# Output tiles with stationary weights: wide and narrow matmuls in series, turned about in every second tile

## The chip, the cores and the metric

The kernel runs on one core of one Trainium2 chip. The metric is the device time of one execution in microseconds (us); lower is better. A core has five engines that work side by side and wait for each other through semaphores: PE (matmul), DVE (vector), ACT (scalar), POOL (general) and SP, which issues transfers here. Each of them works its own instructions off in the order in which they stand in the program.

## What is computed

A decoder trunk of two layers over 256 tokens of width 2048, in float32. Each layer normalises its input, projects it with one wide matrix, runs three groups of attention heads over parts of the result, projects back, and adds; then it normalises again and runs a gated MLP with a short causal convolution. A last norm follows.

```python
for l in range(DEPTH):                                   # DEPTH = 2
    h = _rmsnorm(x, attn_norm[l])
    z = jnp.einsum('bsd,de->bse', h, w_in[l])            # 2048 -> 4934
...
    o_a = _diff_attention(a_q, a_k, a_v, ...)            # 4 heads
    o_b = _mla_attention(m_cq, m_ckv, m_kr, ...)         # 6 heads
    o_c = _forgetting_attention(f_q, f_k, f_v, f_g, ...) # 6 heads
    x = x + jnp.einsum('bsm,md->bsd', mix, w_o[l])
    h = _rmsnorm(x, ffn_norm[l])
    x = x + _conv_gated_mlp(h, ffn_w_up[l], ..., ffn_w_down[l])   # D_FF = 5632
return _rmsnorm(x, final_norm)
```

## The kernel before

The weights, some 400 MB, come through one stream of blocks of 128 x 128 numbers, sixteen blocks a transfer (`load`, tile `raw`, three buffers, issued on SP). `convert` turns eight blocks at a time into two operands of the PE's type for rounded float32: ACT casts the block to `hi` (L134), and DVE subtracts that from the original, which leaves the rest `lo` (L135). Each of `hi` and `lo` has four buffers of eight blocks, and a cast into a buffer waits until PE has read the last block out of it. Activations are split the same way: `hx[k]` holds the high part of 256 tokens in its left half and the low part in its right half, 128 x 512 in all.

`mm_t` makes one output tile of 128 features by 256 tokens over the 16 blocks of its inner dimension, with the weights as the stationary operand. For each block it runs a **wide** matmul, `hi` against all 512 columns of `hx[k]` (left half: high by high, right half: high by low), and a **narrow** one, `lo` against the 256 columns of the high part. They alternate: wide, narrow, wide, narrow (L184, L185), and only the last block has the narrow one first (L187, L188). `total` then adds the two halves of the bank: ACT copies one out (L229), DVE adds the other (L231). `mm_t2` makes two output tiles at once in the same way; it is used for the first tiles of a stage, while the operands still come in (L202 to L205). `mm_v` has the activations stationary and moves 512 columns of weights (L220 to L222, all of one width), for values, the output projection and the second half of the MLP (`residual`). `narrow`, in the latent heads, moves 256 columns of activations against stationary weights (L731 to L733).

`weights(b)` hands out the operands of block `b`; at the first block of a buffer it also calls `convert` for that buffer and the next two, and `load` for two chunks ahead. Background work, such as the heads' scores and softmax, is cut into steps (`bg`, `tick`) that are put between tiles. A scheduler in the library sets the order of each engine's instructions from the program text and the dependences; nothing of a time is written down by hand.

At the start the first chunks come in quarters, and ACT and DVE turn about between converting weights and splitting `x` into `hx` (L361, L362). At the end the last `residual` multiplies three of four column groups of x by the final gain on POOL and the fourth on DVE (L817), the sums of squares are reduced (L406), ACT takes the square root (L407, which needs its function table loaded), DVE the reciprocal (L408), and ACT and DVE scale the two token halves and send them out (L825 to L828).

Of the kernel before, what the change touches and what calls it, by code (L numbers as in the profile page):

```python
# [10 lines left out]
F32R = mybir.dt.float32r  # L11
I32 = mybir.dt.int32
AF = mybir.ActivationFunctionType
# [45 lines left out]
def kernel(ctx: ExitStack, tc: tile.TileContext, xin, xnat, pos, wstream, cst, par, fin, out):  # L59
# [11 lines left out]
    def nm(s):  # L71
        uid[0] += 1
        return f"{s}_{uid[0]}"

    def slot(dtype=F32):
        return slots.tile([P, 2 * T], dtype, tag="slot", name=nm("slot"))
# [10 lines left out]
    def bank(tag, bufs):  # L87
        return psum.tile([P, 512], F32, tag=tag, name=nm(tag), bufs=bufs)

    def f(ap):  # L90
        return ap.bitcast(F32)
# [18 lines left out]
    def load_first():  # L110
        for c in range(3):
            t = wpool.tile([P, CH * P], F32, tag="raw", name=nm("raw"), bufs=3)
            src = wflat[c * CH * P * P : (c + 1) * CH * P * P].rearrange("(p e) -> p e", p=P)
            for i in range(4):
                a = slice(i * 4 * P, (i + 1) * 4 * P)
                nc.sync.dma_start(t[:, a], src[:, a])
                if c < 2:
                    nc.sync.dma_start(xg[4 * c + i], xin[4 * c + i])
            raws[c] = t

    def convert(s, between=None):
        if s >= len(bounds) or s in subs:
            return
        at, n = bounds[s]
        c = at // CH
        load(c)
        o = (at - c * CH) * P
        src = raws[c][:, o : o + n * P]
        hi = wpool.tile([P, SUB * P], F32R, tag="hi", name=nm("hi"), bufs=4)
        lo = wpool.tile([P, SUB * P], F32R, tag="lo", name=nm("lo"), bufs=4)  # L130
        step = SUB // 2 * P if c < 3 else SUB * P
        for o in range(0, n * P, step):
            a = slice(o, min(o + step, n * P))
            nc.scalar.copy(hi[:, a], src[:, a])  # L134
            nc.vector.tensor_tensor(lo[:, a], src[:, a], f(hi[:, a]), ALU.subtract)  # L135
            if between is not None:
                between()
        subs[s] = (hi, lo)

    def weights(b, n=1):  # L140
        s = sub_of[b]
        at = bounds[s][0]
        if b == at:
            convert(s)
            convert(s + 1)
            convert(s + 2)
            load(b // CH + 1)
            load(b // CH + 2)
        o = (b - at) * P
        hi, lo = subs[s]  # L150
        return hi[:, o : o + n * P], lo[:, o : o + n * P]
# [20 lines left out]
        while bg or active:  # L172
            tick()

    def mm_t(moving, hooks={}, tag="mm", bufs=3):
        ps = bank(tag, bufs)
        k = len(moving)
        for i, mv in enumerate(moving):
            if i in hooks:
                hooks[i]()  # L180
            hi, lo = weights(cb[0])
            cb[0] += 1
            if i < k - 1:
                nc.tensor.matmul(ps, hi, mv, start=(i == 0), stop=False)  # L184
                nc.tensor.matmul(ps[:, :T], lo, mv[:, :T], start=False, stop=False)  # L185
            else:
                nc.tensor.matmul(ps[:, :T], lo, mv[:, :T], start=(i == 0), stop=False)  # L187
                nc.tensor.matmul(ps, hi, mv, start=False, stop=True)  # L188
        return ps
# [52 lines left out]
    nc.scalar.activation(warm, warm, AF.Square)  # L242
    nc.scalar.dma_start(pr[0][:, :Q_CV], par[0, :, :Q_CV])
    load_first()
    nc.sync.dma_start(cs, cst)
    nc.sync.dma_start(pint, pos)
    nc.sync.dma_start(pr[0][:, Q_CV:], par[0, :, Q_CV:])
# [283 lines left out]
    for l in range(DEPTH):  # L531
# [4 lines left out]
        if l == 0:  # L536
            first = mm_t2(hx)
            convert(4)
            convert(5)
            squares()  # L540
            first.append(mm_t(hx))
            first.append(mm_t(hx, {KT // 2: norm.cols}, "s", 2))
        else:
            first = mm_t2(hx, {4: lambda: norm.turn(3), KT // 2: norm.cols})
        rstd = norm.rows("rstd")
# [230 lines left out]
        for half in range(2):  # L776
            acts = []
            for i in range(HALF):
                ft = half * HALF + i
                ys = []  # L780
                if rstd is None:
                    pair = mm_t2(hx, {4: lambda: norm.turn(3), KT // 2: norm.cols})
                    rstd = norm.rows("rstd")
                else:
                    pair = None
                for j in range(2):
                    u = total(pair[j] if pair else mm_t(hx))
                    uu = tmp()
                    nc.gpsimd.tensor_tensor(uu, u, rstd, ALU.mult)  # L789
                    w = Q_CV + (ft + j * FT) * 4  # L790
                    y = tmp()
                    nc.scalar.activation(y, uu, AF.Identity, scale=q_[:, w + 2 : w + 3], bias=q_[:, w + 3 : w + 4])  # L792
                    nc.vector.scalar_tensor_tensor(y[:, 1:], uu[:, : T - 1], q_[:, w + 1 : w + 2], y[:, 1:], ALU.mult, ALU.add)  # L793
                    nc.vector.scalar_tensor_tensor(y[:, 2:], uu[:, : T - 2], q_[:, w : w + 1], y[:, 2:], ALU.mult, ALU.add)  # L794
                    ys.append(y)
                nc.scalar.activation(ys[1], ys[1], AF.Silu)  # L796
                nc.gpsimd.tensor_tensor(ys[0], ys[0], ys[1], ALU.mult)  # L797
                a = slot(F32R)
                to_hl(a, ys[0])
                acts.append(a)  # L800
            if half == 0:
                residual(acts, 0)
            elif l < DEPTH - 1:
                hx = [big.tile([P, 2 * T], F32R, tag=f"h{k}", name=nm("h")) for k in range(KT)]
                norm = RowNorm(pr[l + 1][:, Q_AN : Q_AN + KT], hx)
                residual(acts, 0, norm.turn)
            else:
                gf = [slot() for _ in range(4)]
                for j in range(4):
                    nc.sync.dma_start(gf[j], fin[:, j * 512 : (j + 1) * 512])  # L810
                norm = RowNorm(None, None)

                def gain(j):
                    a = slice(j * 512, (j + 1) * 512)
                    for t in range(2):
                        e = nc.vector if j == 3 else nc.gpsimd
                        e.tensor_tensor(xr[t][:, a], xr[t][:, a], gf[j], ALU.mult)  # L817

                residual(acts, 0, gain)
                gain(3)  # L820

    col = norm.cols()
    for j in range(4):
        a = slice(j * 512, (j + 1) * 512)
        nc.vector.tensor_scalar(xr[0][:, a], xr[0][:, a], col[:, 0:1], None, ALU.mult)  # L825
        nc.sync.dma_start(out[0][:, a], xr[0][:, a])
        nc.scalar.activation(xr[1][:, a], xr[1][:, a], AF.Copy, scale=col[:, 1:2])
        nc.scalar.dma_start(out[1][:, a], xr[1][:, a])  # L828


def _layout(inputs):
# [129 lines left out]
```

## Time and profile before

| what | value |
|---|---|
| median of three runs | 2270.15 us (2269.72 to 2270.17) |
| profiled execution | 2270.36 us |
| its span, first to last instruction | 2268.6 us |
| PE busy, share of the span | 2248.8 us, 99% |
| DVE, ACT, POOL busy | 1506.2, 1229.3, 385.1 us |
| matmuls | 12072 |
| mean transfer rate | 182 GB/s |

A timeline row has the start in us from the span's beginning, the duration in us, the engine, the line of the kernel, the operation, output and inputs, and how many follow each other; in brackets stands how long the engine was idle before it and what ended that. A group's row has the count, the busy time in us and the mean duration in ns of one. A row of waits has the waiting engine with tile and line, what it waited for, the total in us, the count and the longest. Matmuls overlap in the pipeline, so a matmul's duration is longer than the distance from its start to the next one's; where PE is concerned, starts are compared.

### The profile page before, as it was taken

The page shows a single profiled execution, that of the slowest core. Times are in us where ns is not written, and L with a number is a line of the kernel's source. Part 1 is how long each engine was busy: PE and PEld are TensorE (multiplying, and loading weights), DVE is VectorE, ACT ScalarE, POOL GpSimd, SP SyncE. Part 2 cuts the span into 40 slices and gives each one's busy share as a digit, 9 for nine tenths or more (in the row PEclk, how much of TensorE's full clock was granted, in tenths as well). Part 3 has the DMA queues.
Part 4 walks back from the last instruction along what each step waited for, and adds up shares of the span by engine and source line. Part 5 has one row for each costly group of instructions (what it writes and reads, how often), then busy time and mean ns, then how long its engine had stood idle before and what let it go on. Part 6 is the DMA issues. An engine that isn't in the chain of part 4 may idle for free.

```text
span 2268.6 us, 31133 instructions
## 1 busy us (share of the span) xinstructions
PE 2248.8 (99%) x12072; PEld 1923.5 (85%) x12072; DVE 1506.2 (66%) x2316; ACT 1229.3 (54%) x1866; POOL 385.1 (17%) x395
## 2 busy tenths in 40 slices
PE   8999999999999999999999999999999999999997
PEld 7888978888888888888888888788888888888886
DVE  8768766777754577775574777567777546777654
ACT  7456645655543455554454665456555435555543
POOL 4600000222210122220050100002222001222110
PEclk9999999999999999999999999999999999999999
DMA  8544435555555555555555444345555555555553
GB/s 310 192 154 165 152 141 182 180 187 187 187 194 187 192 187 188 187 188 190 185 186 185 151 166 162 128 177 186 186 186 186 198 191 188 185 188 185 208 197 120
DMA packets 60771, 413.58 MB, mean 182 GB/s; under 512 B 6864, under 2 KB 6992, under 8 KB 11600
## 3 DMA queue, kind: packets, MB, share of 16 engines
q1 hardware_dynamic: 59904, 410.54, 50.2%
q8 instruction: 94, 1.54, 0.3%
q10 hardware_dynamic: 720, 1.07, 0.1%
q14 instruction: 53, 0.43, 0.1%
HBM read 409.49 MB, written 2.10 MB: 181 GB/s over the span
## 4 chain that ended last, share of the span: by engine, by line
PE 98%; DVE 1%; ACT 0%; DMA 0%; issue 0%; POOL 0%; ACTq 0%; SPq 0%; DVEq 0%
PE mm L184 35%; PE mm L185 18%; PE mm L220 12%; PE mm L222 11%; PE mm L221 11%; PE mm L188 2%; PE s L438 2%; PE mm L205 1%; PE mm L187 1%; PE mm L203 1%; PE pv L470 1%; PE s L397 0%; PE mm L731 0%; PE mm L732 0%; PE mm L733 0%; PE pv L471 0%
## 5 line engine op out<-in xcount | busy, mean ns | idle before, releaser
L135 DVE TENSOR_TENSOR lo<-raw,hi 128x1024 fp32r<-128x1024 f32 (+1 forms) x775 | 988.5, 1276 | 520.6 <-ACT hi L134 516.2
L184 PE MATMUL mm<-h,hi 128*128 128x512 f32 x3375 | 1203.9, 399 | 0.0
L134 ACT CAST hi<-raw 128x1024 fp32r<-128x1024 f32 (+1 forms) x775 | 808.2, 1044 | 588.6 <-PE mm L222 379.4
L185 PE MATMUL mm<-h,lo 128*128 128x256 f32 x3375 | 947.1, 281 | 0.0
L184 PEld LDWEIGHTS mm<-h,hi 128*128 128x128 f32 x3375 | 634.1, 188 | 148.5 <-issue 1.7
L185 PEld LDWEIGHTS mm<-h,lo 128*128 128x128 f32 x3375 | 637.1, 189 | 9.5
L220 PE MATMUL mm<-hi,slot 128*128 128x512 f32 x992 | 388.1, 391 | 0.6 <-DVE slot L735 0.6
L221 PE MATMUL mm<-lo,slot 128*128 128x512 f32 x992 | 384.8, 388 | 0.0
L222 PE MATMUL mm<-hi,slot 128*128 128x512 f32 x992 | 384.7, 388 | 0.0
L789 POOL TENSOR_TENSOR tmp<-tmp,rstd 128x256 f32<-128x256 f32 x176 | 133.2, 757 | 1018.6 <-DVE tmp L231 862.3
L220 PEld LDWEIGHTS mm<-hi,slot 128*128 128x128 f32 x992 | 186.3, 188 | 42.5 <-issue 4.0
L222 PEld LDWEIGHTS mm<-hi,slot 128*128 128x128 f32 x992 | 186.3, 188 | 38.3
L221 PEld LDWEIGHTS mm<-lo,slot 128*128 128x128 f32 x992 | 186.4, 188 | 36.9
L229 ACT COPY tmp<-mm 128x256 f32<-128x256 f32 (+1 forms) x233 | 86.6, 372 | 157.1 <-PE mm L188 155.5
L797 POOL TENSOR_TENSOR tmp<-tmp,tmp 128x256 f32<-128x256 f32 x88 | 119.9, 1362 | 262.1 <-ACT tmp L796 262.1
L792 ACT ACTIVATE tmp<-tmp,par 128x256 f32<-128x256 f32 x176 | 105.7, 601 | 72.1 <-POOL tmp L789 72.0
L231 DVE TENSOR_TENSOR tmp<-mm,tmp 128x256 f32<-128x256 f32 (+1 forms) x233 | 97.7, 419 | 51.1 <-ACT tmp L229 51.0
L476 DVE TENSOR_TENSOR slot<-tmp,slot 128x256 fp32r<-128x256 f32 x96 | 40.8, 425 | 92.2 <-ACT slot L475 92.2
L475 ACT CAST slot<-tmp 128x256 fp32r<-128x256 f32 x96 | 39.0, 406 | 107.3 <-POOL tmp L797 105.5
L188 PE MATMUL mm<-h,hi 128*128 128x512 f32 x225 | 89.8, 399 | 0.0
L794 DVE SCALAR_TENSOR_TENSOR tmp<-tmp,par,tmp 128x254 f32<-128x254 f32 x176 | 85.1, 483 | 6.1
L793 DVE SCALAR_TENSOR_TENSOR tmp<-tmp,par,tmp 128x255 f32<-128x255 f32 x176 | 83.3, 474 | 5.3 <-ACT tmp L792 5.3
(183 smaller groups left out, 1692.4 us busy)
## 6 DMA issues: line engine op xcount, KB each, us to landing
raw<-in_w SPq DMA_DIRECT2D x381, 1024.0 KB, 4.8
raw<-in_w SPq DMA_DIRECT2D x12, 256.0 KB, 5.4
slot<-in_x SPq DMA_DIRECT2D x8, 256.0 KB, 5.2
x<-in_xn SPq DMA_DIRECT2D x2, 1024.0 KB, 10.8
slot<-in_fin SPq DMA_DIRECT2D x4, 256.0 KB, 6.3
out<-x SPq DMA_DIRECT2D x4, 256.0 KB, 3.8
out<-x ACTq DMA_DIRECT2D x4, 256.0 KB, 3.8
raw<-in_w SPq DMA_DIRECT2D x1, 512.0 KB, 3.2
```

The source lines that it names most:

```text
L134: nc.scalar.copy(hi[:, a], src[:, a])
L135: nc.vector.tensor_tensor(lo[:, a], src[:, a], f(hi[:, a]), ALU.subtract)
L184: nc.tensor.matmul(ps, hi, mv, start=(i == 0), stop=False)
L185: nc.tensor.matmul(ps[:, :T], lo, mv[:, :T], start=False, stop=False)
L188: nc.tensor.matmul(ps, hi, mv, start=False, stop=True)
L220: nc.tensor.matmul(ps[t][:, :n], s_hi, hi, start=(i == 0), stop=False)
L221: nc.tensor.matmul(ps[t][:, :n], s_hi, lo, start=False, stop=False)
L222: nc.tensor.matmul(ps[t][:, :n], s_lo, hi, start=False, stop=(i == k - 1))
L231: nc.vector.tensor_tensor(u[:rows], ps[:rows, :T], t[:rows], ALU.add)
L789: nc.gpsimd.tensor_tensor(uu, u, rstd, ALU.mult)
L792: nc.scalar.activation(y, uu, AF.Identity, scale=q_[:, w + 2 : w + 3], bias=q_[:, w + 3 : w + 4])
L797: nc.gpsimd.tensor_tensor(ys[0], ys[0], ys[1], ALU.mult)
```

## The change

`mm_t` first fetches the weights of all its 16 blocks. Then it runs the 16 wide matmuls as one series and the 16 narrow ones as another. In every second tile it is turned about: one wide matmul, which starts the bank, then the 16 narrow ones, then the other 15 wide ones. `hi` and `lo` get a fifth buffer each, and a scratch area of the program is made smaller. The old `mm_t` goes on under the name `mm_first` for two tiles of layer 0. Two smaller edits go with it: 18 matmuls of zeros into a bank that nothing reads, written ahead of the first work, and another division of the end, where a square root of a dummy is written ahead of the last column group, and the final gain of the fourth group is fused with its scaling on DVE.

```diff
-        hi = wpool.tile([P, SUB * P], F32R, tag="hi", name=nm("hi"), bufs=4)
-        lo = wpool.tile([P, SUB * P], F32R, tag="lo", name=nm("lo"), bufs=4)
+        hi = wpool.tile([P, SUB * P], F32R, tag="hi", name=nm("hi"), bufs=5)
+        lo = wpool.tile([P, SUB * P], F32R, tag="lo", name=nm("lo"), bufs=5)
...
-    def mm_t(moving, hooks={}, tag="mm", bufs=3):
+    turn_of = [0]
+
+    def mm_t(moving):
+        ps = bank("mm", 3)
+        k = len(moving)
+        ws = []
+        for i in range(k):
+            ws.append(weights(cb[0]))
+            cb[0] += 1
+        flip = turn_of[0] % 2
+        turn_of[0] += 1
+
+        def high(part):
+            for i in part:
+                nc.tensor.matmul(ps, ws[i][0], moving[i], start=(i == 0), stop=bool(flip and i == k - 1))
+
+        n = 1 if flip else k
+        high(range(n))
+        for i in range(k):
+            nc.tensor.matmul(ps[:, :T], ws[i][1], moving[i][:, :T], start=False, stop=(not flip and i == k - 1))
+        high(range(n, k))
+        return ps
+
+    def mm_first(moving, hooks={}, tag="mm", bufs=3):
...
     load_first()
+    heat = slot(F32R)
+    nc.vector.memset(f(heat), 0.0)
+    hot = bank("pv", 1)
+    for i in range(18):
+        nc.tensor.matmul(hot, heat[:, :P], heat, start=(i == 0), stop=(i == 17))
...
-            first.append(mm_t(hx))
-            first.append(mm_t(hx, {KT // 2: norm.cols}, "s", 2))
+            first.append(mm_first(hx))
+            first.append(mm_first(hx, {KT // 2: norm.cols}, "s", 2))
...
                 def gain(j):
                     a = slice(j * 512, (j + 1) * 512)
+                    if j == 2:
+                        nc.scalar.activation(warm, warm, AF.Sqrt)
                     for t in range(2):
-                        e = nc.vector if j == 3 else nc.gpsimd
-                        e.tensor_tensor(xr[t][:, a], xr[t][:, a], gf[j], ALU.mult)
+                        nc.gpsimd.tensor_tensor(xr[t][:, a], xr[t][:, a], gf[j], ALU.mult)
 
                 residual(acts, 0, gain)
-                gain(3)
...
+        if j == 3:
+            nc.vector.scalar_tensor_tensor(x, x, c, gf[3], ALU.mult, ALU.mult)
+        elif t == 0:
+            nc.vector.tensor_scalar(x, x, c, None, ALU.mult)
+        else:
+            nc.scalar.activation(x, x, AF.Copy, scale=c)
+        (nc.sync, nc.scalar)[t].dma_start(out[t][:, a], x)
...
-    nc = bacc.Bacc("TRN2", target_bir_lowering=False, num_devices=1)
+    nc = bacc.Bacc("TRN2", target_bir_lowering=False, num_devices=1, dynamic_dma_scratch_size=1024)
```

What this does to the order is seen at two places. A row has the line of the kernel that it belongs to (the changed program's lines are its own), the operation, the output and the inputs, and the output's size; the numbers in the names tell buffers apart.

First, PE in the MLP of layer 0, in the midst of an output tile before (`mm` is the output tile, `h` the activations, `hi` and `lo` the two operands of the weights):

```order
L185 MATMUL mm_4654<-h_3601,lo_4573 128x256
L184 MATMUL mm_4654<-h_3602,hi_4610 128x512
L185 MATMUL mm_4654<-h_3602,lo_4611 128x256
L184 MATMUL mm_4654<-h_3603,hi_4610 128x512
L185 MATMUL mm_4654<-h_3603,lo_4611 128x256
L184 MATMUL mm_4654<-h_3604,hi_4610 128x512
```

and in the changed program at the seam of two tiles, from a tile with the wide series first to a turned one, on PE:

```order
L194 MATMUL mm_4564<-h_3631,lo_4517 128x256
L194 MATMUL mm_4564<-h_3632,lo_4517 128x256
L194 MATMUL mm_4564<-h_3633,lo_4517 128x256
L194 MATMUL mm_4564<-h_3634,lo_4517 128x256
L189 MATMUL mm_4622<-h_3619,hi_4516 128x512
L194 MATMUL mm_4622<-h_3619,lo_4517 128x256
```

and sixteen rows on, where the turned tile goes over from its narrow series to the 15 wide ones:

```order
L194 MATMUL mm_4622<-h_3632,lo_4570 128x256
L194 MATMUL mm_4622<-h_3633,lo_4570 128x256
L194 MATMUL mm_4622<-h_3634,lo_4570 128x256
L189 MATMUL mm_4622<-h_3620,hi_4516 128x512
L189 MATMUL mm_4622<-h_3621,hi_4516 128x512
L189 MATMUL mm_4622<-h_3622,hi_4516 128x512
```

Where wide and narrow changed places with every row, one wide matmul now stands between two narrow series, and 15 wide ones run on into the 16 of the tile after.

Second, the start of the program. PE in the first pair of tiles (`mm_t2`, now L225 to L228) of the changed program, where the 18 new matmuls (L272, into the bank `pv`) stand:

```order
L226 MATMUL mm_214<-h_149,lo_185 128x256
L228 MATMUL mm_214<-h_149,hi_184 128x512
L226 MATMUL mm_215<-h_149,lo_185 128x256
L228 MATMUL mm_215<-h_149,hi_184 128x512
L272 MATMUL pv_116<-slot_114 128x512 x18
L226 MATMUL mm_214<-h_150,lo_185 128x256
L228 MATMUL mm_214<-h_150,hi_184 128x512
```

They follow forty matmuls of `mm_t2`, and 24 of it follow them. Their operand's memset (L269) stands on DVE between the splits of the eleventh and twelfth block of x (L390, before L362). ACT at the start of the changed program:

```order
L266 DMA par_73<-in_par 128x42
L265 ACT_TABLE_LOAD
L265 ACTIVATE small_87<-small_87 128x4
L844 ACT_TABLE_LOAD
L844 ACTIVATE small_87<-small_87 128x4
L134 CAST hi_156<-raw_91 128x512
```

The dummy's square root (L844) and a table load moved here from the end of the program text, ahead of the first cast; at the end of ACT's order, the square root of the last norm still has a table load of its own in front of it.

More of the change, by code (lines that the diff above doesn't have):

```diff
@@ L814, in gain, with put @@
                     a = slice(j * 512, (j + 1) * 512)
+                    if j == 2:
+                        nc.scalar.activation(warm, warm, AF.Sqrt)
                     for t in range(2):
-                        e = nc.vector if j == 3 else nc.gpsimd
-                        e.tensor_tensor(xr[t][:, a], xr[t][:, a], gf[j], ALU.mult)
+                        nc.gpsimd.tensor_tensor(xr[t][:, a], xr[t][:, a], gf[j], ALU.mult)
                 residual(acts, 0, gain)
-                gain(3)
     col = norm.cols()
-    for j in range(4):
[L824 to L828, printed above, removed]
+    def put(t, j):
+        a = slice(j * 512, (j + 1) * 512)
+        x, c = xr[t][:, a], col[:, t : t + 1]
+        if j == 3:
[5 more added lines that the diff above has]
+        (nc.sync, nc.scalar)[t].dma_start(out[t][:, a], x)
+    for j in range(4):
+        for t in range(2):
+            put(t, j)
 def _layout(inputs):
```

## The prediction

> **What bounds the kernel now.** I read the page's busy times and its chain first, then who waits for whom, then the groups, and last single matmuls in the timeline.
>
> ```profile
> PE 2248.8 (99%) x12072; PEld 1923.5 (85%) x12072; DVE 1506.2 (66%) x2316; ACT 1229.3 (54%) x1866; POOL 385.1 (17%) x395
> PE 98%; DVE 1%; ACT 0%; DMA 0%; issue 0%; POOL 0%; ACTq 0%; SPq 0%; DVEq 0%
> PE mm L202 <- DVE h L362: 6.7, 1, 6.7
> PE mm L220 <- DVE slot L735: 0.6, 1, 0.6
> PE misc L326 <- ACT rcol L330: 0.2, 1, 0.2
> ```
>
> The first two lines are the page's; the other three are everything that PE ever waited for: the first operands (6.7 us) and 0.8 us later on. So the time is the matmul stream itself plus a head and a tail, and a change counts by what it does to the distance from one matmul's start to the next one's. Busy time doesn't show that, since matmuls overlap:
>
> ```profile
> L184 PE MATMUL mm<-h,hi 128*128 128x512 f32 x3375 | 1203.9, 399 | 0.0
> L188 PE MATMUL mm<-h,hi 128*128 128x512 f32 x225 | 89.8, 399 | 0.0
> ```
>
> A wide matmul is listed with 399 ns, yet they follow each other faster. The second row also counts the tiles: one L188 for each call of mm_t (one record is missing). By the loops there are 226 calls: in layer 0 eleven for the forgetting heads (the first two of them become mm_first and stay as they are), 8 for the differential heads, 8 for the latents, 86 in the MLP; in layer 1 11 + 8 + 8 + 86. **224 tiles change**, each of 16 wide and 16 narrow matmuls. ACT copies each tile out when its last matmul is done, which gives the tile's period:
>
> ```profile
> 1195.12 1.05 ACT L134 CAST hi<-raw 128x1024 fp32r<-128x1024 f32 x1 [1.77 <-PE mm L184]
> 1196.71 0.37 ACT L229 COPY tmp<-mm 128x256 f32<-128x256 f32 x1 [0.55 <-PE mm L188]
> 1197.95 1.05 ACT L134 CAST hi<-raw 128x1024 fp32r<-128x1024 f32 x1 [0.86 <-PE mm L184]
> ...
> 1202.37 0.37 ACT L229 COPY tmp<-mm 128x256 f32<-128x256 f32 x1 [0.55 <-PE mm L188]
> ...
> 1208.02 0.37 ACT L229 COPY tmp<-mm 128x256 f32<-128x256 f32 x1 [0.55 <-PE mm L188]
> ```
>
> (1208.02 - 1196.71) / 2 = 5.655 us a tile, 0.3534 us a pair of one wide and one narrow.
>
> **The series.** What a wide costs behind a wide, and a narrow behind a narrow, stands in other stages of the same trace. First the output projections, 30 wide matmuls in a row, then the narrow ones of the latent projections, 66 in a row (first and last row of each):
>
> ```profile
> 2249.38 0.39 PE L220 MATMUL mm<-hi,slot 128*128 128x512 f32 x1
> ...
> 2255.96 0.39 PE L222 MATMUL mm<-hi,slot 128*128 128x512 f32 x1
> 1399.06 0.28 PE L731 MATMUL mm<-slot,lo 128*128 128x256 f32 x1
> ...
> 1406.86 0.28 PE L733 MATMUL mm<-slot,hi 128*128 128x256 f32 x1
> ```
>
> Wide: 6.58 us / 29 = 0.2269. Narrow: 7.80 / 65 = 0.1200. Together 0.347, against 0.3534 in alternation. Where the two kinds meet, at the end of an MLP half:
>
> ```profile
> 641.33 0.40 PE L184 MATMUL mm<-h,hi 128*128 128x512 f32 x1
> 641.56 0.28 PE L185 MATMUL mm<-h,lo 128*128 128x256 f32 x1
> 641.68 0.40 PE L184 MATMUL mm<-h,hi 128*128 128x512 f32 x1
> 641.92 0.28 PE L185 MATMUL mm<-h,lo 128*128 128x256 f32 x1
> 642.04 0.28 PE L187 MATMUL mm<-h,lo 128*128 128x256 f32 x1
> 642.16 0.40 PE L188 MATMUL mm<-h,hi 128*128 128x512 f32 x1
> 642.40 0.40 PE L220 MATMUL mm<-hi,slot 128*128 128x512 f32 x1
> 642.63 0.39 PE L221 MATMUL mm<-lo,slot 128*128 128x512 f32 x1
> ...
> 643.54 0.39 PE L222 MATMUL mm<-hi,slot 128*128 128x512 f32 x1
> ```
>
> Behind a narrow, the first two wides take (642.63 - 642.16) / 2 = 0.235; from the third on (four intervals, 642.63 to 643.54) it is 0.2275. So the surcharge of some 8 ns sits on the first two wides behind a narrow. In alternation every wide is a first one.
>
> The new order of two tiles is 16 wide, 16 narrow, 1 wide, 16 narrow, 15 wide, and those 15 run on into the next tile's 16: a run of 31, two runs of 16 narrow and a lone wide. 31 x 0.2269 + 2 x 0.008 = 7.050; 32 x 0.120 = 3.840; the lone wide 0.235. Sum 11.125 for two tiles, 5.562 for one, 0.092 less than 5.655. **224 x 0.092 = 20.7 us saved.** A tile of the attention stages, whose neighbours are score matmuls, has one switch more or less; at 8 ns or so that is nothing. The rows to two digits leave 1 ns open on each kind, 224 x 16 x 2 ns = 7 us to either side.
>
> **The 18 extra matmuls.** They are written ahead of the work, but the order of the changed program has them behind the fortieth real one, since their operand's memset stands on DVE behind eleven of the L362 steps. The rows of before at that place:
>
> ```profile
> 8.34 0.63 PE L205 MATMUL mm<-h,hi 128*128 128x512 f32 x1
> 8.98 0.63 PE L205 MATMUL mm<-h,hi 128*128 128x512 f32 x1
> 12.82 0.41 PE L205 MATMUL mm<-h,hi 128*128 128x512 f32 x1
> 13.23 0.87 DVE L362 SCALAR_TENSOR_TENSOR h<-slot,par,h 128x256 fp32r<-128x256 f32 x2
> 16.31 0.39 PE L205 MATMUL mm<-h,hi 128*128 128x512 f32 x1
> 16.54 0.27 PE L203 MATMUL mm<-h,lo 128*128 128x256 f32 x1
> 16.65 0.40 PE L205 MATMUL mm<-h,hi 128*128 128x512 f32 x1
> ```
>
> The wide at 16.31 is the fortieth (counted by weight loads), so the 18 come in at 16.54. By then a pair takes 0.34 (16.31 to 16.65), not the 0.64 of the start (8.34 to 8.98): the wide at 12.82 is the first short one, so PE has its full pace already, and there is nothing left to warm. The memset is done by then: the two steps at 13.23 are the eleventh and twelfth of the sixteen, and between them it takes something from 0 to 0.69 (a 512-column DVE operation, in the last rows below). PE did not wait in this stretch, so all 18 x 0.227 = **4.1 us are added**. Bounds: 0, if the operands of the following steps were late anyway; 18 x 0.42 = 7.6 if zeros ran at the slow pace of the start (two thirds of the 0.64). I take 4.1, the row beside it.
>
> The Trainium skill, page "TensorE: Matmul & The Clock Gate", section on the HAM clock gate, has the array at half clock until it was busy for one window of about 3.4 us. The trace agrees in kind, at 6.1 us (first matmul at 6.7, full pace at 12.8). Had the 18 stood in front, the (12.82 - 6.7) / 0.64, nearly ten, slow pairs could have gained 10 x 0.3 = 3 us; the order takes that away.
>
> **ACT at the start.** The early Sqrt is not tied to anything late, and the order has it in front of the first cast, with a table load:
>
> ```profile
> 1.17 1.28 ACT L242 ACT_TABLE_LOAD   x1 [1.17 <-PEq L950]
> 2.47 0.20 ACT L242 ACTIVATE small<-small 128x4 f32<-128x4 f32 x1
> 4.88 0.62 ACT L134 CAST hi<-raw 128x512 fp32r<-128x512 f32 x1 [2.21 <-DMA raw<-in_w]
> ```
>
> 1.28 + 0.20 = 1.48 fit into the 2.21 in which ACT waits for the first weights: 0. Without that cover it would be 1.5. The first norm's own table load goes, off PE's path.
>
> **The tail.**
>
> ```profile
> 2257.84 1.28 ACT L407 ACT_TABLE_LOAD   x1
> 2259.14 0.30 ACT L407 ACTIVATE rcol<-rcol,cs 128x2 f32<-128x2 f32 x1
> 2257.18 1.37 DVE L817 TENSOR_TENSOR x<-x,slot 128x512 f32<-128x512 f32 x2
> 2258.47 0.15 DVE L406 TENSOR_REDUCE rcol<-sums 128x2 f32<-128x8 f32 x1
> 2259.74 1.67 DVE L825 TENSOR_SCALAR x<-x,rcol 128x512 f32<-128x512 f32 x4
> ```
>
> The two L817 go, and the reduce comes some 0.5 us earlier. But the table load at 2257.84 is still in the order of the changed program, and the square root waits for it until 2259.12 as before: the next thing late is already there. Behind it DVE has three scalings (0.42 each) and two fused ones (between 0.42 and 2 x 0.44 by the 256-column L362), done 2.1 to 3.0 us after 2259.74, where ACT had its fourth scaling before. I take 0, with -0.5 to +0.5.
>
> **Conversions.** A cast waits for PE to leave a buffer (1.77 and 0.86 above), so conversion runs as far ahead as four buffers let it: three blocks of eight pairs, 3 x 8 x 0.353 = 8.5 us, less the cast (1.05) and the subtraction behind it, about as long: some 6 us. In a turned tile the second block's narrow operand is wanted after 0.23 + 8 x 0.12 = 1.2 us instead of 2.8: 1.6 earlier. The fifth buffer gives one block more ahead. Cost 0.
>
> **Sum**, against the profiled execution (2270.36, span 2268.6, 0.2 over the median of 2270.15): 2270.36 - 20.7 + 4.1 + 0 + 0 = **2253.8 us**.
>
> **Rivals.** (1) *The surcharge belongs to the operands.* All runs at 0.227 have the weights as moving operand; in mm_t the wide matmul moves the activations, and always took about 0.235. If it stays so, and the narrow ones take the 0.120 of their run, a tile costs 16 x 0.355 = 5.68: 0.025 more, 224 x 0.025 + 4.1 = 9.7 us slower, **2280**. It decides where the wide takes 232 ns in its run (saving per pair then 4.1 us / 3584 = 1.1 ns). For it: no row shows such a run. Against: at 642.40 a wide that moves weights pays the surcharge too, so it goes by place; and the narrow rows hold 0.120 with weights stationary. 6%. (2) *Each matmul has its price whatever stands beside it*: a pair stays 0.353, only the 18 count, **2274.5**, no change by the bound below. Against it: 0.235 and 0.2275 in neighbouring rows of one kind. 6%. The Trainium skill (same page, section "Back-to-back issue gap") has the gap as N / 2.4 + 2.5 ns, 215.8 and 109.2, without regard to neighbours; by that rule nothing is saved and 3.9 is added, and the trace's 226.9, 120 and 353 disagree with it. (3) *PE meets late conversions* in the 112 turned tiles: 0.1 us in each costs 11.2 us, 2265; from 0.15 on all is lost. Against: 4 us of lead. 4%. (4) *The 18 are free* because the operands of the steps behind them were about to be late: **2249.7**. For: DVE has hardly a pause there. Against: PE never waited. 6%.
>
> **Numbers.** Forecast 78%; rivals 6, 6, 4 and 6. What can be told from no change is about 0.2%, 4.5 us. Faster: forecast, (4), half of (3): 0.86. Same: (2) and a little: 0.06. Slower: (1) and the rest: 0.08. The range takes in 7 us of cadence below, and above that together with the slow pace of the 18 and light conversion waits: 2246 to 2266.
>
> **What would show it.** In the profile after: runs of wide matmuls of mm_t starting 0.227 apart and narrow ones 0.120; two tile copies 11.12 apart in the MLP; 18 matmuls from 16.5 to 20.6; first cast at 4.9; the square root's table load still in the tail; PE waiting for ACT or DVE under 2 us in all. A wide run at 0.235 makes it wrong by (1); new lines of PE waiting for L134 or L135 by (3).

## The result and the profile after

The changed kernel takes **2304.36 us** (median of four runs, 2303.50 to 2304.63). The kernel before took 2270.16 beside it (2269.72 to 2270.47). The ratio is 1.015, with an interval of 1.0133 to 1.0168: the change makes the kernel 34 us slower. The forecast was 2253.8, the range 2246 to 2266. The profiled execution took 2304.31 us, its span is 2302.5.

The page after, PE's busy time and the shares of the chain that ended last:

```profile
PE 2246.5 (98%) x12090; PEld 1934.1 (84%) x12090; DVE 1472.0 (64%) x2316; ACT 1205.4 (52%) x1866; POOL 414.5 (18%) x395
PE 78%; DVE 11%; ACT 5%; POOL 4%; issue 2%; DMA 0%; ACTq 0%; POOLq 0%; DVEq 0%; SPq 0%
```

PE still looks 98% busy, but the chain is no longer PE's alone: a fifth of it runs through DVE, ACT and POOL, where it was 98% PE before. What PE waits for (total us, count, longest):

```profile
PE mm L194 <- DVE lo L135: 31.4, 32, 1.0
PE mm L225 <- DVE h L390: 6.7, 1, 6.7
PE mm L243 <- DVE tmp L254: 4.6, 2, 2.3
```

The second row is the old wait for the first operands. The other two are new: 32 waits of a narrow matmul for `lo`, and two for a bank that an evacuation (the adding of a finished tile's halves) gives back late. Two single waits of 1.2 and 0.2 us in the attention stages are left out here. To see where they fall, the time is cut into stages (distance from the first weight load of a stage to that of the next, us). The last column is the run e9 below.

| stage | before | after | one row moved (e9) |
|---|---|---|---|
| first pair of tiles (mm_t2); after and in e9 with the 18 matmuls | 13.80 | 17.55 | 17.16 |
| layer 0, MLP, first half: 42 tiles | 237.12 | 253.24 | 234.17 |
| its residual | 119.70 | 122.21 | 119.60 |
| layer 0, MLP, second half: 44 tiles | 248.73 | 264.84 | 245.43 |
| its residual | 122.38 | 126.53 | 122.28 |
| layer 1, MLP, first half: 42 tiles | 237.22 | 234.12 | 234.12 |
| layer 1, MLP, second half: 44 tiles | 248.73 | 245.37 | 245.37 |
| all else | 1040.9 | 1038.7 | 1038.5 |

Layer 1 gained as forecast in kind; layer 0's MLP lost 16.1 in each half, and 2.5 and 4.2 more in the residuals behind. One turned tile of that stage, on PE:

```profile
910.49 2.08 PE L194 MATMUL mm<-h,lo 128*128 128x256 f32 x16
912.40 0.40 PE L189 MATMUL mm<-h,hi 128*128 128x512 f32 x1
912.63 1.60 PE L194 MATMUL mm<-h,lo 128*128 128x256 f32 x12
915.24 0.74 PE L194 MATMUL mm<-h,lo 128*128 128x256 f32 x4 [1.01 <-DVE lo L135]
```

Twelve narrow matmuls run at 0.120 from 912.63, so the thirteenth would start at 914.07. It starts at 915.24, 1.17 later. Its operand comes from the third of the buffers that this tile reads (the tiles of layer 0 begin in the middle of an eight-block buffer). This recurs every 12.40 us (the last matmul ahead of such a wait starts at 477.2, 489.6 and 502.0, for instance), where PE's own work for two tiles is 11.15. So something else needs 12.40 us for two tiles. One such round on the three other engines, ACT first, then DVE, then POOL:

```profile
925.28 1.04 ACT L134 CAST hi<-raw 128x1024 fp32r<-128x1024 f32 x1
...
928.76 0.60 ACT L820 ACTIVATE tmp<-tmp,par 128x256 f32<-128x256 f32 x1 [1.23 <-POOL tmp L817]
...
933.92 0.60 ACT L820 ACTIVATE tmp<-tmp,par 128x256 f32<-128x256 f32 x1 [3.35 <-POOL tmp L817]
934.43 1.04 ACT L134 CAST hi<-raw 128x1024 fp32r<-128x1024 f32 x1
935.66 0.42 ACT L824 ACTIVATE tmp<-tmp 128x256 f32<-128x256 f32 x1 [0.19 <-DVE tmp L822]
937.36 0.41 ACT L503 CAST slot<-tmp 128x256 fp32r<-128x256 f32 x1 [1.28 <-POOL tmp L825]
937.67 1.05 ACT L134 CAST hi<-raw 128x1024 fp32r<-128x1024 f32 x1
```

```profile
926.36 1.22 DVE L135 TENSOR_TENSOR lo<-raw,hi 128x1024 fp32r<-128x1024 f32 x1 [0.52 <-ACT hi L134]
927.50 0.42 DVE L254 TENSOR_TENSOR tmp<-mm,tmp 128x256 f32<-128x256 f32 x1
929.40 0.48 DVE L821 SCALAR_TENSOR_TENSOR tmp<-tmp,par,tmp 128x255 f32<-128x255 f32 x1 [1.48 <-ACT tmp L820]
929.92 0.48 DVE L822 SCALAR_TENSOR_TENSOR tmp<-tmp,par,tmp 128x254 f32<-128x254 f32 x1
930.32 2.36 DVE L135 TENSOR_TENSOR lo<-raw,hi 128x1024 fp32r<-128x1024 f32 x2
932.59 0.42 DVE L254 TENSOR_TENSOR tmp<-mm,tmp 128x256 f32<-128x256 f32 x1
934.56 0.48 DVE L821 SCALAR_TENSOR_TENSOR tmp<-tmp,par,tmp 128x255 f32<-128x255 f32 x1 [1.55 <-ACT tmp L820]
935.08 0.48 DVE L822 SCALAR_TENSOR_TENSOR tmp<-tmp,par,tmp 128x254 f32<-128x254 f32 x1
935.50 1.23 DVE L135 TENSOR_TENSOR lo<-raw,hi 128x1024 fp32r<-128x1024 f32 x1
```

```profile
928.00 0.73 POOL L817 TENSOR_TENSOR tmp<-tmp,rstd 128x256 f32<-128x256 f32 x1 [3.06 <-DVE tmp L254]
933.16 0.73 POOL L817 TENSOR_TENSOR tmp<-tmp,rstd 128x256 f32<-128x256 f32 x1 [4.43 <-DVE tmp L254]
936.16 1.17 POOL L825 TENSOR_TENSOR tmp<-tmp,tmp 128x256 f32<-128x256 f32 x1 [2.27 <-ACT tmp L824]
```

Read by start times, each row is released by the one before it on another engine, or stands behind it on its own: cast (925.28), its subtraction L135 and the evacuation L254 behind it on DVE (926.36, 927.50), product with rstd L817 on POOL (928.00), L820 on ACT (928.76), L821 and L822 and then **two** subtractions on DVE (929.40 to 932.68), the next tile's evacuation L254 (932.59), L817, L820, L821 and L822 again (933.16 to 935.56), L824 on ACT (935.66), the gate product L825 on POOL (936.16 to 937.33, drawn out by the subtraction that DVE runs beside it), L503 on ACT (937.36), and then the cast at 937.67, with which the round begins anew. From 925.28 to 937.67 it is 12.39 us, and PE stands nowhere in it. The knot is the last step: on ACT the third buffer's cast stands behind L503, which waits for POOL's product of the tile pair before. A cast of weights, which depends on no activation, so waits for the whole epilogue, and the next epilogue's evacuation waits behind that cast's subtraction on DVE.

In layer 1, where the tiles begin at the start of a buffer, ACT's order is another:

```profile
1667.62 0.42 ACT L824 ACTIVATE tmp<-tmp 128x256 f32<-128x256 f32 x1 [0.19 <-DVE tmp L822]
1667.95 1.04 ACT L134 CAST hi<-raw 128x1024 fp32r<-128x1024 f32 x1
1669.33 0.41 ACT L503 CAST slot<-tmp 128x256 fp32r<-128x256 f32 x1 [0.34 <-POOL tmp L825]
```

There a cast stands between L824 and L503, uses the time in which POOL multiplies, and PE never waits.

That place alone does not make the round too long. In layer 0's MLP of the kernel before, a cast stands behind the same copy (there L475, with the product L797 ahead of it), first on ACT, then on DVE:

```profile
902.08 1.05 ACT L134 CAST hi<-raw 128x1024 fp32r<-128x1024 f32 x1 [1.27 <-PE mm L184]
...
905.01 0.41 ACT L475 CAST slot<-tmp 128x256 fp32r<-128x256 f32 x1 [1.02 <-POOL tmp L797]
905.32 1.04 ACT L134 CAST hi<-raw 128x1024 fp32r<-128x1024 f32 x1
```

```profile
905.79 0.42 DVE L231 TENSOR_TENSOR tmp<-mm,tmp 128x256 f32<-128x256 f32 x1
906.40 1.71 DVE L135 TENSOR_TENSOR lo<-raw,hi 128x1024 fp32r<-128x1024 f32 x1 [0.19 <-ACT hi L134]
```

But there the evacuation of the next tile (L231) stands ahead of that cast's subtraction on DVE and not behind it, and another cast of the same round waits 1.27 for PE: the round has slack. It is the order of all rows together that became too long.

### The profile page after: what moved, and what is told of

It reads as the page before. It is cut to its first block, busy times and chain, and to the rows that moved or that the text cites. A ratio compares the mean times of both kernels' runs of the same rounds, so it can differ in the third digit from the quotient of the medians.

```text
span 2302.5 us, 31046 instructions
## 1 busy us (share of the span) xinstructions
PE 2246.5 (98%) x12090; PEld 1934.1 (84%) x12090; DVE 1472.0 (64%) x2316; ACT 1205.4 (52%) x1866; POOL 414.5 (18%) x395
## 4 chain that ended last, share of the span: by engine, by line
PE 78%; DVE 11%; ACT 5%; POOL 4%; issue 2%; DMA 0%; ACTq 0%; POOLq 0%; DVEq 0%; SPq 0%
PE mm L189 23%; PE mm L194 12%; PE mm L243 11%; PE mm L245 11%; PE mm L244 11%; DVE lo L135 6%; POOL tmp L817 2%; ACT tmp L820 2%; POOL tmp L825 2%; ACT hi L134 2%; PE s L466 2%; DVE tmp L821 2%; PE mm L228 1%; DVE tmp L254 1%; DVE tmp L822 1%
## 5 line engine op out<-in xcount | busy, mean ns | idle before, releaser
L135 DVE TENSOR_TENSOR lo<-raw,hi 128x1024 fp32r<-128x1024 f32 (+1 forms) x775 | 950.3, 1235 | 443.5 <-ACT hi L134 399.9
L189 PE MATMUL mm<-h,hi 128*128 128x512 f32 x3584 | 862.5, 392 | 0.0
L189 PEld LDWEIGHTS mm<-h,hi 128*128 128x128 f32 x3584 | 664.8, 188 | 134.1 <-ACT tmp L252 1.3
L194 PEld LDWEIGHTS mm<-h,lo 128*128 128x128 f32 x3584 | 462.2, 190 | 51.6 <-DVE lo L135 38.0
L194 PE MATMUL mm<-h,lo 128*128 128x256 f32 x3584 | 473.7, 284 | 31.4 <-DVE lo L135 31.4
L817 POOL TENSOR_TENSOR tmp<-tmp,rstd 128x256 f32<-128x256 f32 x176 | 188.7, 1072 | 1078.1 <-DVE tmp L254 923.4
L820 ACT ACTIVATE tmp<-tmp,par 128x256 f32<-128x256 f32 x176 | 105.9, 602 | 355.1 <-POOL tmp L817 355.1
L821 DVE SCALAR_TENSOR_TENSOR tmp<-tmp,par,tmp 128x255 f32<-128x255 f32 x176 | 85.0, 483 | 212.8 <-ACT tmp L820 212.7
L825 POOL TENSOR_TENSOR tmp<-tmp,tmp 128x256 f32<-128x256 f32 x88 | 93.4, 1062 | 205.3 <-ACT tmp L824 205.3
L254 DVE TENSOR_TENSOR tmp<-mm,tmp 128x256 f32<-128x256 f32 (+1 forms) x233 | 97.4, 418 | 0.6 <-ACT tmp L252 0.5
L822 DVE SCALAR_TENSOR_TENSOR tmp<-tmp,par,tmp 128x254 f32<-128x254 f32 x176 | 85.1, 483 | 6.2
L503 ACT CAST slot<-tmp 128x256 fp32r<-128x256 f32 x96 | 39.0, 406 | 67.2 <-POOL tmp L825 65.6
L243 PE MATMUL mm<-hi,h 128*128 128x512 f32 (+1 forms) x192 | 68.3, 356 | 0.0
```

What stands on the lines that cost most here:

```text
L189: nc.tensor.matmul(ps, ws[i][0], moving[i], start=(i == 0), stop=bool(flip and i == k - 1))
L194: nc.tensor.matmul(ps[:, :T], ws[i][1], moving[i][:, :T], start=False, stop=(not flip and i == k - 1))
L243: nc.tensor.matmul(ps[t][:, :n], s_hi, hi, start=(i == 0), stop=False)
L254: nc.vector.tensor_tensor(u[:rows], ps[:rows, :T], t[:rows], ALU.add)
```

## The experiments

Every figure is a median beside runs of the kernel before on the same chip (2269.97 to 2270.21).

**e1, without the 18 matmuls.** The lines of `heat` and `hot` are left out, nothing else.

```diff
-    for i in range(18):
-        nc.tensor.matmul(hot, heat[:, :P], heat, start=(i == 0), stop=(i == 17))
```

> The changed kernel without the 18 extra matmuls and their memset. The order of layer 0's MLP is the same row for row. If the 18 cost what their rows in the profile after show (the first pair of tiles took 17.55 us where it took 13.80 before), the time falls by 3.7 to 4.1 us, to about 2300.4. If the operands behind them were late anyway, it stays at 2304.

Measured: 2299.94 us, ratio 1.0133 (1.0117 to 1.0148), 4.4 less than the changed kernel. The layer 0 halves stay at 253.21 and 264.90. The 18 cost what they occupy and have nothing to do with the loss in layer 0's MLP.

**e2, half of the gate product.**

```diff
-                nc.gpsimd.tensor_tensor(ys[0], ys[0], ys[1], ALU.mult)
+                nc.gpsimd.tensor_tensor(ys[0][:, : T // 2], ys[0][:, : T // 2], ys[1][:, : T // 2], ALU.mult)
```

> The gate's product on POOL is made for 128 of 256 columns only; the other half is left out of the computation. The order on every engine is the same row for row. Theory A (layer 0's MLP goes at the pace of one chain through ACT, DVE and POOL, 12.40 us for two tiles, in which this product stands once with 1.17 us): the period falls by what the product loses, 0.4 to 0.6 us, to 11.8 to 12.0, the wait of PE in a turned tile from 1.18 to 0.6 to 0.8 us, and the time by about 20 us, to 2280 to 2289. Theory B (the converted blocks come late because the five buffers are given back too late): the product is in no one's way, 2304 as it is.

Measured: 2292.66 us, 1.0098 (1.0081 to 1.0114). The total missed the expected 2280 to 2289, since the product did not halve. All executions of it, min/median/max in ns, in the changed kernel and in this one:

```profile
L825 POOL TENSOR_TENSOR tmp<-tmp,tmp x88: 737/1167/1340, 417.0 to 2175.3; 128x256 f32<-128x256 f32 x88
```

```profile
L825 POOL TENSOR_TENSOR tmp<-tmp,tmp x88: 460/889/1057, 416.7 to 2165.0; 128x128 f32<-128x128 f32 x88
```

The median fell by 0.28, and the period from 12.40 to 12.11, by 0.29: one for one. The product lies on the chain, and the mechanism holds though the size was wrong.

**e3, tiles aligned to the buffers.** Four blocks of zeros are put into the weight stream ahead of each MLP and skipped, so that layer 0's tiles begin at the start of a buffer too.

```diff
+        cb[0] += 4
...
+        blocks.append(np.zeros((4, P, P), f32))
```

> Four blocks of zeros are put ahead of each layer's MLP in the weight stream and skipped, so that in both layers an output tile of the MLP begins at the beginning of a buffer, as it does in layer 1 now; the order in layer 0's MLP becomes another. Theory A: the chain there gets about as short as in layer 1 (11.15 to 11.3 us for two tiles), and the 39 us of layer 0's MLP go: about 2262 to 2268. Theory B says the same, since a tile then holds two buffers and not three. If the place of the tiles in the buffers has no part in it, 2304 stays.

Measured: 2285.51 us, 1.0067 (1.0052 to 1.0082); 2262 to 2268 was expected, a miss. The waits are 27 of about 0.74 by the starts of matmuls and come before the last eight narrow matmuls instead of the last four; the period is 11.96. So the odd start of the tiles is not the cause by itself: the order that comes out here has a long round too. On ACT the cast even stands ahead of L503 here (911.95 and 912.90), as in layer 1, so there is more than one way to close a round that is too long.

**e4, no tile turned.**

```diff
-        flip = turn_of[0] % 2
+        flip = 0
```

> No tile is turned about: 16 wide, 16 narrow, in all 224. By the starts in the profile after, a wide series of 16 behind a narrow one takes 3.67 us and a narrow one 1.91, 5.59 for a tile against 5.653 before and 5.576 turned, which alone would be 2 us slower than turned. If the late operands come only from the turned tiles, whose narrow operands are wanted early, PE's waits go and the time is 2262 to 2268; if they come from the chain through ACT, DVE and POOL, it depends on that chain's order, and waits of PE stay where its period is over 11.17 us.

Measured: 2296.77 us, 1.0118 (1.0103 to 1.0133). In the layer 0 halves hardly anything waits any more for `lo` (4.1 us in all) and they take 237.13 and 248.92, but what the chain is behind is paid at the start of each residual, 5.1 us at the longest:

```profile
PE mm L243 <- DVE tmp L254: 17.1, 4, 5.1
...
PE mm L194 <- DVE lo L135: 4.1, 11, 0.4
```

and layer 1 waits here too (its last residual with the tail takes 138.04 instead of 131.97). So it is not the early demand of turned tiles (rival 3 as it was put) that costs the time: with no tile turned most of the loss is there. Not all of it is waiting. Behind three of the four waits for a bank, PE at first runs at about half its pace (wide matmuls start 0.43 apart from 654.76 on, 0.23 elsewhere in this stage), which adds 6.7 us to the 17.1. The changed kernel has this once, behind the second of its waits for a bank, and loses 1.6 us by it.

**e5, the product with rstd on DVE.**

```diff
-                    nc.gpsimd.tensor_tensor(uu, u, rstd, ALU.mult)
+                    nc.vector.tensor_tensor(uu, u, rstd, ALU.mult)
```

> The changed kernel with the MLP's scaling by the norm (L817, twice in the chain of two tiles, 0.73 us each on POOL) put on DVE, behind the sum that it waits for; ACT's order stays row for row. Theory A: each step shrinks to DVE's 0.42 and loses the hand-over to POOL and its share of the one to ACT, so two tiles take 11.5 to 11.8 us instead of 12.40, the wait in a turned tile falls to 0.3 to 0.6 us, and the time to 2275 to 2287. Theory B: DVE gets more work and nothing less to wait for, so 2304 or more.

Measured: 2270.61 us, 1.0002 (0.9993 to 1.0011), less than expected. The period is 11.61, as expected, and the waits of 1.17 have become 0.39. DVE, the busier engine, got 176 more operations, and the kernel is 34 us faster. From the start of L254 to that of L820 it is now 0.92, twice in each round, where it was 1.26 and 1.33; 0.31 of each difference is the shorter operation (0.42 instead of 0.73), and little is the hand-over.

**e6, both products on DVE, without the 18 matmuls.** The same edit for the gate product as well, and e1's.

> The changed kernel without the 18 extra matmuls and with both POOL steps of the MLP's chain (the scaling and the gate's product) on DVE. Theory A: the chain gets shorter than the 11.15 us that PE needs for two tiles, PE no longer waits in layer 0's MLP, and its two halves gain 3.1 and 3.4 us against before, as layer 1's do now; with the attention stages about even and the small gains of the head and tail that is 2255 to 2259, faster than before by 0.5 to 0.7%. Theory B: PE still waits in layer 0, 2290 to 2300.

Measured: **2253.8 us**, 0.9928 (0.9911 to 0.9945). PE waits for nothing in the MLP; the layer 0 halves take 234.16 and 245.43. The time lies a little below the 2255 to 2259 that were expected. This run does not show that the shorter steps alone do it, because the scheduler also made another order of them: on ACT a cast now stands ahead of the gated tile's copy (907.24 and 908.20) and waits for PE.

**e7, both products on DVE in the kernel before; e8, five buffers in the kernel before.** Two controls: the first puts e6's two products on DVE, the second takes only the fifth `hi` and `lo` and the smaller scratch area.

> The kernel before with the same two POOL steps on DVE. If e6 is fast because the series need fewer nanoseconds and the chain lets them, the kernel before, which never waits, gains nothing from a shorter chain: 2270 within 1 us. If e6 owes its gain to the DVE steps as such, this kernel gains as much.

> The kernel before with five buffers for each operand and the smaller scratch area, and nothing else of the change. If the buffers alone lengthen the chain by the order that the scheduler makes with them, PE waits here too and the time is over 2275; if it takes the series' order to do that, 2270 within 1 us.

Measured: e7 2269.31 us, 0.9996 (0.9987 to 1.0006); e8 2268.40, 0.9993 (0.9983 to 1.0002). By these intervals neither can be told from the kernel before. All ten executions of each lie below the 25 of the kernel before, though, and e8 is a little below what was expected; in the profiles the first pair of tiles is shorter (12.98 and 12.68 us instead of 13.80) and the tail by 0.3. In the MLP's stages nothing changes by more than 0.2 us: the products on POOL cost nothing there, and the buffers bring no waits.

**e9, one row moved.** The test of the knot itself: the copy of a gated tile to its rounded high half (L503) is written one pair later and tied behind the last cast on ACT; with it goes the subtraction on DVE. PE's and POOL's rows are in the same order as in the changed kernel, and the 18 matmuls are there.

```diff
-            nc.scalar.copy(hi[:, a], src[:, a])
+            casts.append(nc.scalar.copy(hi[:, a], src[:, a]).ins)
...
-                    u = total(pair[j] if pair else mm_t(hx))
+                    ps = pair[j] if pair else mm_t(hx)
+                    if late and j == 1:
+                        with tc.issue_after(casts[-1]):
+                            to_hl(*late.pop())
+                    u = total(ps)
...
-                to_hl(a, ys[0])
+                late.append((a, ys[0]))
```

> The changed kernel with one row moved on ScalarE and one on VectorE in each pair of MLP tiles: the copy of the gated tile to its rounded high half (and the subtraction for its low half) stands behind the third buffer's cast instead of ahead of it. TensorE's and GpSimd's rows are the same. Theory A (the period of 12.40 us is a closed chain, because the third buffer's cast stands in ScalarE's order behind a row that waits for GpSimd's gate product): the product (1.17), its hop and the copy (about 1.5 us together) leave the chain, which then needs about 10.9 us for two tiles against TensorE's 11.15; waits before the last narrow operands fall from 1.3 us to under 0.2, the two layer 0 MLP halves fall to 234 to 240 and 245 to 252 us, and the kernel takes 2258 to 2275 us. Rival B (the engines' work is simply too long beside each other, wherever the row stands): the period stays at 12 us or more, and the kernel over 2290. Between them (period 11.3 to 11.9) a second chain is next, as when the first product was moved off GpSimd.

Measured: **2258.70 us**, 0.9950 (0.9935 to 0.9964), 45.7 less than the changed kernel. ACT in the same stage (L830 is the old L824, L505 the old L503):

```profile
922.03 0.42 ACT L830 ACTIVATE tmp<-tmp 128x256 f32<-128x256 f32 x1
922.74 1.05 ACT L136 CAST hi<-raw 128x1024 fp32r<-128x1024 f32 x1 [0.29 <-PE mm L191]
923.69 0.36 ACT L254 COPY tmp<-mm 128x256 f32<-128x256 f32 x1
923.95 0.41 ACT L505 CAST slot<-tmp 128x256 fp32r<-128x256 f32 x1
```

The cast now follows L830, and what it waits for is PE (0.29): the round is open, and conversion runs ahead as far as the buffers let it. L505 finds its product done and waits for nothing. PE's waits in the whole program, beside the first operands, are

```profile
PE pv L500 <- ACT slot L495: 1.2, 1, 1.2
PE misc L371 <- DVE tmp L364: 0.2, 1, 0.2
```

**e10, zeros truly first.** e6 with 13 matmuls of zeros at the front of PE's order, their memset on POOL.

```diff
+    heat = slot(F32R)
+    nc.gpsimd.memset(f(heat), 0.0)
+    hot = bank("pv", 1)
+    for i in range(13):
+        nc.tensor.matmul(hot, heat[:, :P], heat, start=(i == 0), stop=(i == 12))
```

> The kernel without GpSimd in the MLP's chain (2253.8 us), with 13 matmuls of zeros at the very front of TensorE's order, ahead of all real ones, their zeros written by GpSimd at the start. If what costs time in the first pair of tiles is that TensorE's first microseconds run at half pace whatever it does, these matmuls take that time while nothing else is ready: the first pair falls from 12.6 to about 10.5 us, the kernel to 2251 to 2252.5. If the first pair is bounded by its data (transfers, casts, first operands), it stays at 12.6 and the kernel at 2253.5 to 2254.5; if the zeros end after the first operands are ready, it is later by as much, up to 2256.

Measured: 2253.63 us, 0.9927 (0.9911 to 0.9944), the same as e6. PE at its start, and the end of the first pair of tiles:

```profile
1.31 5.07 PE L271 MATMUL pv<-slot 128*128 128x512 f32 x13 [1.31 <-POOL slot L268]
6.82 0.50 PE L225 MATMUL mm<-h,hi 128*128 128x512 f32 x1 [0.44 <-DVE h L390]
7.15 0.28 PE L226 MATMUL mm<-h,lo 128*128 128x256 f32 x1
...
18.06 0.73 PE L228 MATMUL mm<-h,hi 128*128 128x512 f32 x2 [0.29 <-DVE h L390]
```

The real matmuls do run at full pace from the second on, and still the pair takes 12.27 against 12.59: towards its end PE's weight loads stand idle at four places between 15.4 and 18.1 us, 1.1 us in all; the longest, at 18.06, is a wait for the splits of x. What the pace gave, the operands took back for the most part.

**e11, e9 without the 18 matmuls.** e9's and e1's edits together.

> The kernel with the moved row (2258.7 us), without the 18 matmuls of zeros at the start. What is left of the change is the turned series of every second tile, with nothing waiting. If the 18 cost what the first pair of tiles shows (17.16 us with them, 12.6 to 13.8 without), the kernel takes 2254 to 2255.5 us; if the removal of the 18 gains nothing because TensorE's half pace then falls on real matmuls, it stays above 2257.

Measured: 2254.67 us, 0.9931 (0.9915 to 0.9948), 4.0 less than e9. With the row moved, what is left of the change brings 15.4 us, 12.7 of them in the MLP's tiles.

## Why the prediction was wrong

**Conversions: the step that failed.** "conversion runs as far ahead as four buffers let it … some 6 us … Cost 0." This lead was read from rows of before in which casts waited for PE (1.77, 0.86); they are of layer 1's attention projections, and the MLP's rows, in which casts stand behind rows that wait for POOL, were not used. It presumed that casts are bounded by PE alone and go on being so. In the changed program the rows of ACT and DVE stand in another order, and the cast behind L503 is bounded by the epilogue (the work from evacuation to gated tile) of the tile pair before, and the next evacuation by that cast's subtraction; the round through ACT, DVE and POOL needs 12.40 us, more than PE. No amount of buffers gives a lead when the producer's own round is longer than the consumer's: the first waits come at 465 to 477 us, some five pairs into the stage, when the lead is used up. Shown: shortening a link by 0.28 shortens the round by 0.29 (e2), making two links shorter on DVE shortens it by 0.79 (e5), and moving the one cast ahead of L503 ends every wait of PE in the MLP and gives back 45.7 us (e9). The order of PE and of the start was followed in the changed program, ACT's and DVE's in the MLP was not.

**Rival 3** named PE waiting for conversions and had 4%. Its reason, the turned tiles' earlier demand, was not the cause (e4), and its price, some 0.1 us in 112 tiles, was far from 1.2 in 30 of the 43 turned tiles of layer 0's MLP. The 4 us of lead that spoke against it were the wrong term.

**The series: right in kind, too large in size.** Forecast was 11.125 us for two tiles. PE in layer 1 of the changed kernel (the run of 31 wides in two overlapping windows, then what follows it):

```profile
1668.43 2.49 PE L189 MATMUL mm<-h,hi 128*128 128x512 f32 x10
1670.53 5.15 PE L189 MATMUL mm<-h,hi 128*128 128x512 f32 x22
1675.52 2.08 PE L194 MATMUL mm<-h,lo 128*128 128x256 f32 x16
1677.43 0.40 PE L189 MATMUL mm<-h,hi 128*128 128x512 f32 x1
1677.66 2.08 PE L194 MATMUL mm<-h,lo 128*128 128x256 f32 x16
1679.58 1.80 PE L189 MATMUL mm<-h,hi 128*128 128x512 f32 x7
```

It is 11.15 from 1668.43 to 1679.58. The narrow runs take 1.91 and 1.92 (0.120 each) and the lone wide 0.23, as put. The tenth wide of the run starts at 1670.53, so the first nine distances are 0.233 on average, and the 22 from there to 1675.52 are 0.2268: the surcharge behind a narrow run lasts some nine matmuls and costs 0.06 a run, where the prediction had it on two, with 0.016. The four MLP halves of e9 save 12.7 us against before (237.12 + 248.73 + 237.22 + 248.73 - 234.17 - 245.43 - 234.12 - 245.37), 0.074 a tile and not 0.092. In the attention stages the prediction took the neighbours for nothing, and there the runs are short. Behind score matmuls, at 1324.54 in the changed kernel, the second of 16 wides starts 0.42 after the first, and the other 15 distances are 0.229 on average; in the kernel before, the first distance at such a place is 0.34. The stages with these tiles (in layer 0 from the end of the first pair of tiles to the 42 of the MLP, in layer 1 from its first weight load to the same place) took 384.56 and 397.65 us before and take 383.92 and 396.30 in e9: 2.0 us saved in all, where 52 tiles at 0.092 would have been 4.8. The term of 20.7 was some 14.7.

**The 18 matmuls: right.** 4.1 forecast; 4.4 (e1) and 4.0 (e11) measured. But of the 3 us that they were said to be able to gain in front, the first pair shows 0.3 and the time none (e10).

**Start and tail: right.** The first cast starts at 4.86 (4.88 before). The square root's table load is still in the tail (at 2292.12, for 1.28), and the last residual with the tail takes 131.97 against 132.30, within the half microsecond that was left open. The first cast after:

```profile
4.86 0.62 ACT L134 CAST hi<-raw 128x512 fp32r<-128x512 f32 x1 [0.67 <-DMA raw<-in_w]
```

**Rivals 1, 2 and 4** fell: the long runs of wide matmuls settle at 0.227 and not at 0.235, the pairs did become cheaper, and the 18 are not free. With the one row moved, the kernel (2258.7) lies inside the range, 4.9 above the forecast, of which the series' size makes up more than all (20.7 - 14.7 = 6.0); smaller gains in other stages go the other way.

**What stays open.** Why the scheduler makes this order in layer 0 and another in layer 1 was not tried; e3 and e4 show only that other starts and other series give other rounds (11.96 and 11.75), both longer than PE's 11.15. Which link closes the round in those two was not tested.

## What to carry to other kernels

When a change alters the order in which operands are asked for, follow every engine's new order around one full period and not only that of the engine that sets the time: add up the longest closed round through the others, with each hand-over, and compare it with the bound engine's period. A lead read from waits in the old trace holds only as long as the producer is released by the consumer. An instruction that depends on nothing late (a weight cast) should not stand behind one that waits for another engine; here one row's place was worth 45.7 us, 2% of the kernel. But add the round up rather than look for that one sign: in the kernel before a cast stands at the same place and costs nothing, and in e3 it stands ahead and PE still waits.

## What the runs showed of the hardware

The surcharge behind a series of narrow matmuls is a matter of some nine matmuls and not of the first two (0.233 on average against 0.2268 above). In the rows that the prediction read, at 642.63, it is gone after two; those wide matmuls move weights and not activations, and which difference decides is open.

A product of 128x256 on POOL takes 0.73 while DVE is idle (L817 at 928.00; the shortest L825 took 0.737) and 1.17 beside a subtraction of DVE: L135 runs from 935.50 to 936.73, and L825, begun at 936.16, ends at 937.33, 0.60 after it. That fits e2, where half a product saved only 0.28: the wait for the subtraction stayed, and half a product ends 0.32 after it. The Trainium skill, page "SBUF — State Buffer", section "Who interferes with whom", says that a DVE instruction with two SBUF inputs and a GpSimd instruction that reads SBUF exclude each other, the one issued first holding the port to its end. The trace agrees with its 0.60.

When PE gets its full pace differs from profile to profile: 6.1 us after the first matmul in the trace of before, and 3.6 in that of e6 (two wides 0.64 apart at 9.08 and 9.72, and short ones from 10.34 on; first matmul at 6.78):

```profile
9.08 0.63 PE L228 MATMUL mm<-h,hi 128*128 128x512 f32 x1
...
9.72 0.63 PE L228 MATMUL mm<-h,hi 128*128 128x512 f32 x1
...
10.34 0.40 PE L228 MATMUL mm<-h,hi 128*128 128x512 f32 x1
```

First pairs without extra matmuls took from 12.6 to 13.8 us in six profiles. Each is one execution of another program, so how much of this belongs to the execution and how much to the program is open.
